# A tuned matmul-scale-add kernel: one 8-tile store split by partitions into 112, 8 and 8

## The chip, the cores and the metric

One core of a Trainium2 chip. The metric is the device time of one execution in microseconds; the kernel is launched once. Executions of the kernel before agree within about 0.4% in one set of rounds, so several timed rounds of both kernels on the same chip are compared.

## The reference

```python
batch, m, k, n = 16, 512, 1024, 768          # all float32
def reference(x, weight, scale, add_value):  # scale = 0.1
    return (scale * np.matmul(x, weight) + add_value).astype(np.float32)
```

The 8192 rows of `x` are 64 tiles of 128 rows. Read: 32 MiB of `x`, 24 MiB of `add_value`, 3 MiB of weights; written: 24 MiB.

## The kernel before

Everything comes and goes through DMAs between HBM (the main memory) and SBUF (the core's own memory, 128 partitions), which SyncE issues in the order of a list: loads of `x` ("x"), of the weights ("w"), of `add_value` ("a"), and stores of results ("o", then "l" and "r" for the two parts of the last tile). A result overwrites its `add_value` in the buffer `ao` and is stored from there. A partition holds eight consecutive rows of the output for a group of eight tiles, so an 8-tile store writes one run of 24,576 bytes from each of the 128 partitions. From here on such a run, one partition's part of an 8-tile store, is called a row.

```python
STREAM = [
    # ... (cut)
    ("o", 16, 8), ("o", 24, 8), ("a", 48, 8), ("x", 56, 8), ("a", 56, 8), ("o", 32, 8),
    ("o", 40, 8), ("o", 48, 8), ("o", 56, 4), ("o", 60, 1), ("o", 61, 1), ("o", 62, 1),
    ("l", 63, 1), ("r", 63, 1),
]
    # ... (cut)
    out_v = out_f.rearrange("(g p t) n -> p g t n", p=P, t=G)     # P = 128, G = 8
    # ... (cut)
        else:
            while done["step"] <= last:
                step()                       # compute up to this tile
            k = s % A_SLOTS
            n0, n1 = {"o": (0, N), "l": (0, CUT), "r": (CUT, N)}[op]
            nc.sync.dma_start(rows(out_v, s, n)[:, :, n0:n1], ao[:, k:k + n, n0:n1])
```

## Time and profile before

| | before |
|---|---|
| time, median of the first 3 runs | 210.86 us (210.78 to 211.06) |
| span of the profiled run | 209.2 us |
| last compute instruction ends | 204.03 us |
| TensorE busy | 196.4 us (94%) |
| bytes moved | 87.21 MB, 417 GB/s over the span |

Two resources are full nearly to the end, TensorE and the 16 DMA engines, and the last 5 us belong to the DMA engines alone. The prediction shows the lines for that. Here is what it doesn't show: the last 20 us of the kernel before in stretches of 4 us. The columns are named by the header; the last two are the share of time in which the 16 engines had a packet, and what they moved.

```profile
core 0: us, PE busy (x) PEld busy (x) DVE busy (x) ACT busy (x) POOL busy (x), PEclk, DMA share, GB/s
188.00:192.00 4.00, 4.00 (x28) 2.40 (x26) 1.19 (x2) 1.48 (x2) 0.00 (x0) 1.00 0.98 416
192.00:196.00 4.00, 4.00 (x28) 2.47 (x27) 1.68 (x2) 1.01 (x1) 0.00 (x0) 1.00 1.00 430
196.00:200.00 4.00, 4.00 (x29) 2.61 (x28) 0.96 (x1) 1.28 (x2) 0.00 (x0) 1.00 0.95 406
200.00:204.00 4.00, 3.57 (x22) 1.88 (x20) 2.04 (x3) 0.74 (x1) 0.00 (x0) 1.00 0.96 395
204.00:208.00 4.00, 0.00 (x0) 0.00 (x0) 0.04 (x1) 0.00 (x0) 0.00 (x0) 0.83 0.51 195
```

Read the last two columns as a pair. A share near 1 with 400 to 430 GB/s says that the engines are busy and go at full rate: in this trace a row mostly takes 912 ns, 26.9 GB/s, 431 for 16 engines. Both fall together after 204 us, as engines run out of work.

SyncE's own wait at the end of the program, for the stores to land (us in total, times, longest):

```profile
SPq L293 <- DMA out_dram<-ao: 3.7, 3, 2.8
```

### The profile page before, as it was taken

The page shows a single profiled execution, that of the slowest core. Times are in us where ns is not written, and L with a number is a line of the kernel's source. Part 1 is how long each engine was busy: PE and PEld are TensorE (multiplying, and loading weights), DVE is VectorE, ACT ScalarE, POOL GpSimd, SP SyncE. Part 2 cuts the span into 40 slices and gives each one's busy share as a digit, 9 for nine tenths or more (in the row PEclk, how much of TensorE's full clock was granted, in tenths as well). Part 3 has the DMA queues.
Part 4 walks back from the last instruction along what each step waited for, and adds up shares of the span by engine and source line. Part 5 has one row for each costly group of instructions (what it writes and reads, how often), then busy time and mean ns, then how long its engine had stood idle before and what let it go on. Part 6 is the DMA issues. An engine that isn't in the chain of part 4 may idle for free.

```text
span 209.2 us, 2988 instructions
## 1 busy us (share of the span) xinstructions
PE 196.4 (94%) x1218; PEld 119.5 (57%) x1218; DVE 131.1 (63%) x223; ACT 49.3 (24%) x52; POOL 63.2 (30%) x69
## 2 busy tenths in 40 slices
PE   7599499999999999999999999999999999999990
PEld 2355256656665666566665666565666656666550
DVE  0545413309969969898697886949994994223340
ACT  2513113233103112113032031121130230332310
POOL 1310536420292090503903606303503039100000
PEclk9889979999999999999999999999999999999997
DMA  6999999999999999999999999999999999999993
GB/s 233 418 431 447 423 408 441 451 445 407 404 481 410 418 432 418 432 451 415 437 417 436 436 421 425 442 434 423 423 432 445 445 409 418 432 447 426 409 402 152
DMA packets 5485, 87.21 MB, mean 417 GB/s; under 512 B 608, under 2 KB 736, under 8 KB 2016
## 3 DMA queue, kind: packets, MB, share of 16 engines
q1 hardware_dynamic: 5472, 87.03, 97.7%
q8 instruction: 9, 0.15, 0.3%
q14 instruction: 4, 0.03, 0.0%
HBM read 61.87 MB, written 25.17 MB: 416 GB/s over the span
## 4 chain that ended last, share of the span: by engine, by line
PE 90%; DMA 3%; DVE 2%; ACT 1%; POOL 0%; issue 0%; ACTq 0%; POOLq 0%
PE mm L168 80%; PE tp L146 10%; DMA xs<-in_x_dram 3%; DVE ao L235 1%; ACT xt L152 1%; DVE ao L204 1%; POOL xb L136 0%; DVE xb L132 0%; DVE ao L176 0%; ACTq L152 0%; POOLq L136 0%
## 5 line engine op out<-in xcount | busy, mean ns | idle before, releaser
L168 PE MATMUL mm<-w_bf,xt 128*128 128x512 bf16 (+1 forms) x736 | 130.8, 331 | 0.6 <-DVE ao L204 0.4
L168 PEld LDWEIGHTS <-xt 128*128 128x128 bf16 x736 | 69.6, 99 | 50.8 <-ACT xt L152 11.4
L176 DVE SCALAR_TENSOR_TENSOR ao<-mm,ao 128x768 f32<-128x768 f32 (+2 forms) x62 | 58.3, 944 | 54.1 <-PE mm L168 35.3
L152 ACT COPY xt<-tp 128x1024 bf16<-128x1024 bf16 (+1 forms) x49 | 46.6, 961 | 146.0 <-PE tp L146 146.0
L120 DVE STREAM_TRANSPOSE vt<-vx 32x256 f32<-32x256 f32 x144 | 62.7, 435 | 6.2 <-POOL vx L109 4.0
L136 POOL CAST xb<-xs 128x1024 bf16<-128x1024 f32 x43 | 43.2, 1040 | 56.2 <-DMA xs<-in_x_dram 46.5
L168 PE MATMUL mm<-w_bf,vt 128*128 128x512 bf16 (+1 forms) x288 | 49.7, 326 | 0.0
L168 PEld LDWEIGHTS <-vt 128*128 128x128 bf16 x288 | 28.2, 98 | 17.5
L109 POOL CAST vx<-xs 128x1024 bf16<-128x1024 f32 x18 | 18.3, 1040 | 53.8 <-DVE vt L120 44.7
L146 PE MATMUL tp<-identity,xb 128*128 128x128 f32 x184 | 28.3, 277 | 5.4 <-POOL xb L136 3.0
L146 PEld LDWEIGHTS tp<-identity,xb 128*128 128x128 f32 x184 | 21.7, 143 | 12.1 <-POOL xb L136 3.4
L104 DVE CAST w_bf<-ao 128x768 bf16<-128x768 f32 x8 | 4.1, 557 | 3.8 <-DMA ao<-in_weight_dram 3.8
L132 DVE CAST xb<-xs 128x512 bf16<-128x512 f32 x3 | 1.9, 696 | 5.6 <-DMA xs<-in_x_dram 5.6
L94 PE MATMUL warm<-zeros 128*128 128x512 bf16 x10 | 4.3, 617 | 1.2 <-DVE zeros L82 1.2
L134 POOL CAST xb<-xs 128x512 bf16<-128x512 f32 x2 | 1.6, 834 | 5.5 <-DMA xs<-in_x_dram 5.5
L94 PEld LDWEIGHTS <-zeros 128*128 128x128 bf16 x10 | 1.3, 140 | 3.4 <-issue 2.2
L204 DVE TENSOR_SCALAR ao<-mm 128x768 f32<-128x768 f32 x2 | 1.8, 952 | 2.3 <-PE mm L168 2.3
L235 DVE TENSOR_TENSOR ao<-ao 128x768 f32<-128x768 f32 x3 | 2.7, 950 | 0.0
L134 ACT CAST xb<-xs 128x512 bf16<-128x512 f32 x1 | 0.6, 618 | 4.8 <-DMA xs<-in_x_dram 4.8
L134 ACT ACT_TABLE_LOAD x1 | 1.3, 1283 | 0.7 <-PEq L279 0.7
L201 ACT ACTIVATE ao<-mm 128x768 f32<-128x768 f32 x1 | 0.8, 817 | 0.0
L82 DVE MEMSET zeros<- 128x256 uint32 x1 | 0.3, 272 | 0.9 <-PEq L279 0.9
(6 smaller groups left out, 0.9 us busy)
## 6 DMA issues: line engine op xcount, KB each, us to landing
xs<-in_x_dram SPq DMA_DIRECT2D x6, 4096.0 KB, 27.3
ao<-in_add_value_dram SPq DMA_DIRECT2D x7, 3072.0 KB, 24.3
out_dram<-ao SPq DMA_DIRECT2D x7, 3072.0 KB, 31.2
xs<-in_x_dram SPq DMA_DIRECT2D x3, 2048.0 KB, 22.0
ao<-in_weight_dram SPq DMA_DIRECT2D x4, 768.0 KB, 9.5
xs<-in_x_dram SPq DMA_DIRECT2D x1, 1536.0 KB, 6.0
ao<-in_add_value_dram SPq DMA_DIRECT2D x1, 1536.0 KB, 23.7
out_dram<-ao SPq DMA_DIRECT2D x1, 1536.0 KB, 11.7
```

The source lines that it names most:

```text
L94: nc.tensor.matmul(warm[:, 0:CUT], zeros[:, 0:P], zeros, start=True, stop=True)
L104: nc.vector.tensor_copy(w_bf[:, j + i, :], ao[:, s + i, :])
L109: nc.gpsimd.tensor_copy(vx[:, i, :], xs[:, (t0 + i) % X_SLOTS, :])
L120: nc.vector.transpose(vt[b:b + 32, :, 32 * a:32 * a + 32], pairs[32 * a:32 * a + 32, :, b:b + 32])
L134: other(xb[:, K // 2:K], src[:, K // 2:K])
L136: nc.gpsimd.tensor_copy(xb, src)
L146: nc.tensor.transpose(tp[:, c, :], pairs[:, c * P:(c + 1) * P], identity)
L152: nc.scalar.copy(dst[:, c:c + q, :, :], src[:, c:c + q, :, :])
L168: nc.tensor.matmul(mm_tiles[t, cols[0]][:, n0:n1], lhs(t, j), w_bf[:, j, n0:n1], start=(j == 0), stop=(j == KJ - 1))
L176: nc.vector.scalar_tensor_tensor(a, mm_tiles[t, part][:, n0:n1], float(scale), a, op0=mybir.AluOpType.mult, op1=mybir.AluOpType.add)
L204: nc.vector.tensor_scalar(ao[:, EARLY_AT + t, :], mm_tiles[t, BOTH[0]][:, 0:N], float(scale), None, op0=mybir.AluOpType.mult)
L235: nc.vector.tensor_add(ao[:, t, :], ao[:, EARLY_AT + t, :], ao[:, t, :])
```

## The change

The intent: at the end the 16 engines do not finish together. Engine completions for the three pieces: sixteen for the 112 rows, and eight for each 8-row piece. Shared out equally, that is nine rows of this store for eight engines and seven for the others, to let the others, taken to be late, catch up. The traces give no engine's number. The eight that complete the 8-row pieces are called the lower engines and the others the upper; these are names and say nothing more.

```diff
+SHARED = ("o", 40)
...
-            nc.sync.dma_start(rows(out_v, s, n)[:, :, n0:n1], ao[:, k:k + n, n0:n1])
+
+            cuts = [0, 112, 120, P] if (op, s) == SHARED else [0, P]
+            for p0, p1 in zip(cuts, cuts[1:]):
+                nc.sync.dma_start(
+                    rows(out_v, s, n)[p0:p1, :, n0:n1], ao[p0:p1, k:k + n, n0:n1])
```

## The prediction

> **What bounds the kernel now.** I read the page of the kernel before first: the slices of the span (second part), the DMA queues (third) and the chain that ended last (fourth). Then the waits of the DMA queue, the list of DMA issues with their time to landing, and last the end of the span cut into short stretches.
>
> The slices have all 16 DMA engines busy from the second to the last slice, at about 430 GB/s, and the DMA share of the stretches from 24 us to 180 us is 1.00 to 1.01. The page's queues add that besides the kernel's own transfers nine instruction fetches of 16 KB (q8)[...] ride on the same engines.
>
> ```profile
> DMA  6999999999999999999999999999999999999993
> GB/s 233 418 431 447 423 408 441 451 445 407 404 481 410 418 432 418 432 451 415 437 417 436 436 421 425 442 434 423 423 432 445 445 409 418 432 447 426 409 402 152
> q1 hardware_dynamic: 5472, 87.03, 97.7%
> q8 instruction: 9, 0.15, 0.3%
> q14 instruction: 4, 0.03, 0.0%
> ```
>
> TensorE is 94% busy as well, so two things end close together. Which of them ends last is read at the end of the chain (start, length, what), where the last work is a VectorE instruction:
>
> ```profile
> 199.64 3.95 PE mm L168 x24
> 203.59 0.02 issue
> 203.61 0.42 DVE ao L176
> ```
>
> The chain is over at 204.03 us; the span is 209.2 us. What follows is stores. The reader sees it in the stretches of the tail (length, busy time of PE, PEld, DVE, ACT, POOL, then clock, DMA share, GB/s):
>
> ```profile
> 204.00:205.00 1.00, 0.00 (x0) 0.00 (x0) 0.04 (x1) 0.00 (x0) 0.00 (x0) 1.00 0.94 373
> 205.00:206.00 1.00, 0.00 (x0) 0.00 (x0) 0.00 (x0) 0.00 (x0) 0.00 (x0) 1.00 0.78 293
> 206.00:207.00 1.00, 0.00 (x0) 0.00 (x0) 0.00 (x0) 0.00 (x0) 0.00 (x0) 0.83 0.26 94
> 207.00:208.20 1.20, 0.00 (x0) 0.00 (x0) 0.00 (x0) 0.00 (x0) 0.00 (x0) 0.50 0.05 17
> ```
>
> The share times 16 is the number of engines at work: 15, 12.5, 4, and then 0.8, that is one engine alone. The tail is not short of bandwidth, it waits for one late engine. The trace keeps the 16 completions of each DMA apart (without the engine's number). For the 8-tile store of tiles 48 to 55 they lie, before the last, at 3.45, 3.25, 3.13, 3.00, 2.80, 2.54, then 1.78, 1.77, 1.68, 1.66, 1.64, 1.57, 1.53, 1.29, 1.07 and 0 us. Up to 24.2 us the 16 are within 0.4 us of each other. At each of the nine q8 fetches one more engine falls back by about 1.5 us, and that at 189.9 us pushes one that was already among the last by another 1.3. So six engines lead by 2.5 us or more, and one is alone at the back.
>
> The list of issues says that the last store is not alone on its engines: 4.1 us to landing for one of 128 KB, of which those ahead of it in the queue are most (its first completion came 1.6 us after issue).
>
> ```profile
> out_dram<-ao SPq DMA_DIRECT2D x1, 256.0 KB, 4.4
> out_dram<-ao SPq DMA_DIRECT2D x1, 128.0 KB, 4.1
> ```
>
> [...]
>
> [...]
>
> [...]a row of 24,576 bytes took 912 ns in nearly every packet, 26.9 GB/s, whoever else was at work.[...]
>
> **The change, part by part.** No instruction of TensorE, VectorE, ScalarE or GpSimd changes in kind or order; only the line numbers move. SyncE gets two more issues.
>
> 1. Issue cost: two more at about 0.33 us (the stores' issues took 332 to 431 ns), at 157.8 us, where SyncE then waits until 180.5 for the next tiles. Nothing on the path: 0.
>
> 2. Semaphore slots: eight go round, and two more DMAs shift who shares. The two last stores (issued at 203.5 and 204.1) now come after the 112-row and the first 8-row piece in their slots. The store they replace landed at 193.6, 10 us earlier, so even a late landing by 8 us costs nothing.
>
> 3. Shares, as intended: [...]If the late engine is an upper one, it ends 0.91 us earlier. The next ones lead it by 1.07 to 1.78 us; an engine of the lower half among these, 0.91 later, ends up 0.2 to 0.9 us ahead of the old end. The gain is then 0.2 to 0.9 us, 210.0 to 210.7. If it is a lower one, the end moves out by 0.91 to 211.8.
>
> 4. [...]Together +4.6 to +7 us: 215.5 to 217.9.
>
> **The rivals.** (a) Balance works: item 3 with an upper late engine, about 210.2. For it: the late engines are few, the queue is backlogged up to the end, and whoever chose the lower engines for the extra share probably saw which are late; the ninth fetch fell on one that had been hit before[...]. Against it: item 4, and that the gain is capped by the next engines. (b) Balance the wrong way: 211.8. Nothing in the profile speaks for it in particular, but nothing excludes it, as the completions carry no engine number. (c) [...]215.5 to 217.9[...]. (d) The end hidden anyway: TensorE's chain ends at 204.03 and a store lands some 1.6 us after issue on a free engine, so no balance whatever brings the last landing under about 205.7, against 208.2 now; the most that could ever be won is 2.5 us, 1.2%. This rules out "faster by over 2%".
>
> **Range and chances.** I give [...]rival (a) 0.34, rival (b) 0.08. [...]That gives slower 0.55, same 0.43, faster 0.02. The figure is 216.0 us[...]; the range 209.8 to 221 takes in the balance that works[...], and nothing between is likely.
>
> **What would show it.** Step 3 would be right if packets of 24,576 bytes stay at 912 ns, the stretch from 207 us is gone and the last stores land within about 3.5 us of issue. Step 4 would be right if some 16 or more packets of that size take 3 to 4 us around 188 to 197 us, the GB/s of the last four or five slices fall well below 400, and the last small stores take 8 us or more to landing, with some engines then idle while eight are late. Steps 1 and 2 are wrong if TensorE's chain ends later than 204.1 us or SyncE waits for the store's pieces before the last two issues. The prediction is wrong as a whole if an 8-row piece runs at 27 GB/s for each of its eight engines[...].

Passages are cut from the prediction: the terms of step 4, the grounds of rival (c), and in step 3 how the rows were shared out (one row more for each lower engine, one less for each upper, 0.91 us each way by the trace's row). The sum came to 216.0 us. Step 4 was put at +4.6 to +7 us on top of the 210.9 before, 215.5 to 217.9, with a chance of 0.58; the figure stood in its lower part because rivals (a) and (b), 210.2 and 211.8, lie below it. What step 4 comes down to, and what the runs below test, is that the place of the small pieces costs time, because several engines read a few neighbouring partitions at once.

The fetches that it counts are these in the trace before: nine q8 packets of 16,384 bytes, each 1.0 to 1.1 us. After the first one engine's next completion came at 30.6 us, those of the other 15 by 29.1; after the ninth, at 189.9 us, one engine completed at 193.6 and the next at 192.3.

## The result, and the profile after

The changed kernel takes 219.88 us (median of 4, 218.25 to 220.14) against 210.82 for the kernel before in the same rounds: slower, by a ratio of 1.0417 (95% interval 1.0371 to 1.0463). Here and below a ratio is the mean time of one kernel's fast runs over that of the other's of the same rounds, so it is not quite the ratio of the medians.

The profiled run is the fastest of the changed kernel's, 218.25 us with a span of 216.5 us, so its trace shows some 7.3 us of the loss and not all 9. The slices of the changed kernel's page:

```profile
DMA  6999999999999999999999999999999999999952
GB/s 248 412 425 438 418 426 437 416 456 433 422 430 439 436 427 415 457 415 451 409 422 428 441 431 419 424 431 427 436 450 430 412 422 431 403 282 295 401 237 83
```

Up to the 35th slice the two kernels are alike; then two slices move 282 and 295 GB/s, although the row above still has nines. The same stretches of 4 us as before, for the changed kernel:

```profile
188.00:192.00 4.00, 4.00 (x28) 2.34 (x27) 1.46 (x2) 1.21 (x2) 0.00 (x0) 1.00 1.17 305
192.00:196.00 4.00, 4.00 (x29) 2.60 (x27) 1.42 (x2) 1.01 (x1) 0.00 (x0) 1.00 0.93 270
196.00:200.00 4.00, 4.00 (x28) 2.53 (x27) 0.96 (x1) 1.55 (x2) 0.00 (x0) 1.00 0.84 292
200.00:204.00 4.00, 3.30 (x21) 1.68 (x18) 2.07 (x3) 0.47 (x1) 0.00 (x0) 1.00 0.97 406
204.00:208.00 4.00, 0.00 (x0) 0.00 (x0) 0.00 (x0) 0.00 (x0) 0.00 (x0) 1.00 0.85 346
208.00:212.00 4.00, 0.00 (x0) 0.00 (x0) 0.00 (x0) 0.00 (x0) 0.00 (x0) 0.58 0.41 167
```

From 188 to 200 us the engines have packets (1.17, 0.93 and 0.84; over 1 because a packet counts where it starts) but move only 305, 270 and 292 GB/s. That is not idleness, it is slowness: each packet takes longer. The packet records of the trace show this (they, and the completions below, are read from the trace itself; no view prints them one by one). Before, nine rows in ten took 912 to 920 ns, and only 9 of 1,792 took over 1 us, the longest 1.57. In the changed kernel rows of 1.1 to 2 us begin at 184 us, with the 112-row piece, and twelve rows between 190 and 200 us took 2.7 to 5.3 us.

Twelve us at some 130 GB/s less than the kernel before (416, 430 and 406 against 305, 270 and 292) are 1.5 MB left over, 3.7 us of all 16 engines. But the loss is not shared by all 16. The trace has each engine's completion (without its number). For the store of tile 60 ten engines are done from 202.6 to 206.4 us, and six from 210.1 to 212.7. The two 8-row pieces show eight engine completions each, as was counted on; two engines are through the second piece by 194.3 us, and six only from 198.2 to 200.9. The six late completions of the store behind them (tiles 48 to 55) come 7.3 us after these, 205.5 to 208.2, which is eight rows of 912 ns: they are the same six. Six slow engines set the end, and the others run dry: after 208 us the share is 0.41, six or seven engines of 16.

The chain's last lines in the changed kernel (start, length, what):

```profile
199.37 3.95 PE mm L169 x24
203.34 0.42 DVE ao L177
```

Compute ends at 203.76 us, no later than before. All of the loss comes after it, and SyncE's wait for the stores at the end has grown accordingly:

```profile
SPq L298 <- DMA out_dram<-ao: 10.6, 5, 7.9
```

The times from issue to landing say the same of the small stores behind the split one. Before, then after (KB each, us):

```profile
out_dram<-ao SPq DMA_DIRECT2D x3, 384.0 KB, 7.4
```

```profile
out_dram<-ao SPq DMA_DIRECT2D x3, 384.0 KB, 15.0
out_dram<-ao SPq DMA_DIRECT2D x2, 192.0 KB
out_dram<-ao SPq DMA_DIRECT2D x1, 256.0 KB, 12.1
```

The 192 KB line is the two 8-row pieces; this view gives them no time.

### The profile page after: what moved, and what is told of

Same layout as the page of the kernel before. It is cut to its first block, busy times and chain, and to the rows that moved or that the text cites. A ratio compares the mean times of both kernels' runs of the same rounds, so it can differ in the third digit from the quotient of the medians.

```text
span 216.5 us, 2992 instructions
## 1 busy us (share of the span) xinstructions
PE 195.7 (90%) x1218; PEld 119.3 (55%) x1218; DVE 131.9 (61%) x223; ACT 49.3 (23%) x52; POOL 64.1 (30%) x69
## 4 chain that ended last, share of the span: by engine, by line
PE 67%; DMA 20%; DVE 5%; SPq 1%; issue 1%; ACT 0%; DVEq 0%; ACTq 0%
PE mm L169 60%; DMA ao<-in_add_value_dram 15%; PE tp L147 6%; DMA xs<-in_x_dram 5%; DVE vt L121 3%; DVE ao L177 2%; SPq L103 1%; ACT xt L153 0%; SPq L249 0%; DVEq L177 0%; ACTq L153 0%
## 5 line engine op out<-in xcount | busy, mean ns | idle before, releaser
L137 POOL CAST xb<-xs 128x1024 bf16<-128x1024 f32 x43 | 44.1, 1061 | 55.4 <-DMA xs<-in_x_dram 54.8
L147 PE MATMUL tp<-identity,xb 128*128 128x128 f32 x184 | 28.9, 283 | 5.0 <-DVE xb L133 2.6
L147 PEld LDWEIGHTS tp<-identity,xb 128*128 128x128 f32 x184 | 22.3, 146 | 11.2 <-issue 3.1
L95 PE MATMUL warm<-zeros 128*128 128x512 bf16 x10 | 3.6, 538 | 1.2 <-DVE zeros L83 1.2
L236 DVE TENSOR_TENSOR ao<-ao 128x768 f32<-128x768 f32 x3 | 3.5, 1231 | 0.0
```

The lines of the kernel that those rows point to most:

```text
L95: nc.tensor.matmul(warm[:, 0:CUT], zeros[:, 0:P], zeros, start=True, stop=True)
L137: nc.gpsimd.tensor_copy(xb, src)
L147: nc.tensor.transpose(tp[:, c, :], pairs[:, c * P:(c + 1) * P], identity)
L236: nc.vector.tensor_add(ao[:, t, :], ao[:, EARLY_AT + t, :], ao[:, t, :])
```

## The experiments

The theory ("neighbours"): several engines that read a few neighbouring partitions at the same time slow each other, so the place of the small pieces is the cost. Rivals: the engines' shares themselves are the cost (the lower eight carry too much); or the number of DMAs, their issues and their semaphore slots (in the trace before eight semaphores, used in turn, tell of the landings).

In the expectations the terms for this theory are cut; the figure behind a cut is what it came to. Cut as well are its opposites: extra_spread as slow as the packed run, extra_spread_up as fast as the spread run; of that for extra_four_ports the figure is left, 211.8.

All twelve kernels are the kernel before with an edit at the store of tiles 40 to 47.

| run | the store of tiles 40 to 47 | median us | before us | ratio (95% interval) |
|---|---|---|---|---|
| the change | 112 + 8 + 8 rows | 219.88 | 210.82 | 1.0417 (1.0371 to 1.0463) |
| tiles_4_2_2 | 4 + 2 + 2 tiles, 128 rows each | 211.00 | 211.21 | 0.9995 (0.9982 to 1.0008) |
| rows_112_16 | 112 + 16 rows | 214.36 | 211.21 | 1.0138 (1.0113 to 1.0163) |
| rows_64_64 | 64 + 64 rows | 216.33 | 211.21 | 1.0243 (1.0227 to 1.0259) |
| rows_8_8_112 | 8 + 8 + 112 rows | 215.94 | 211.03 | 1.0240 (1.0221 to 1.0258) |
| rows_112_only | 112 rows, the rest left out | 212.47 | 211.01 | 1.0074 (1.0061 to 1.0087) |
| shares_only | shares 9 and 7, 8-row pieces from every fourth partition | 210.95 | 211.01 | 0.9998 (0.9986 to 1.0010) |
| extra_spread | whole, and 2 x 8 rows, every fourth of partitions 0 to 29 | 211.73 | 211.03 | 1.0046 (1.0034 to 1.0059) |
| extra_spread_up | the same, every fourth of partitions 64 to 93 | 212.11 | 211.03 | 1.0063 (1.0045 to 1.0081) |
| extra_four_ports | the same, every second of partitions 0 to 15 | 213.57 | 211.01 | 1.0123 (1.0108 to 1.0138) |
| extra_low | the same, 8 neighbours each, partitions 0 to 15 | 213.43 | 211.01 | 1.0121 (1.0107 to 1.0135) |
| extra_packed | the same, 8 neighbours each, partitions 112 to 127 | 218.61 | 211.03 | 1.0359 (1.0346 to 1.0372) |
| extra_mid | the same, 8 neighbours each, partitions 64 to 79 | 219.24 | 210.93 | 1.0394 (1.0380 to 1.0408) |

What a run reads stands in the second column. A difference in us below is the ratio less 1, times the time before.

### Is it the number of DMAs? (tiles_4_2_2)

```diff
-            nc.sync.dma_start(rows(out_v, s, n)[:, :, n0:n1], ao[:, k:k + n, n0:n1])
+            cuts = [0, 4, 6, 8] if (op, s) == ("o", 40) else [0, n]
+            for t0, t1 in zip(cuts, cuts[1:]):
+                nc.sync.dma_start(
+                    rows(out_v, s + t0, t1 - t0)[:, :, n0:n1], ao[:, k + t0:k + t1, n0:n1])
```

> The same store cut into three DMAs as well, but by tiles (4, 2 and 2), each over all 128 partitions: the same number of issues and the same semaphore slots as in the change[...]. [...]within 0.5 us of before (210.3 to 211.3). Theory that the number of DMAs, the issues or the slots cost the 9 us: about 219. Shares theory (lower engines overloaded): 210.8, so this run parts only the count from the rest.

Measured: 0.9995, no difference, and no row of an 8-tile store over 1 us near the end. Three DMAs in the place of one, with the same shift of semaphore slots, cost nothing. That rival is out.

### Equal shares, fewer partitions (rows_112_16, rows_64_64)

```diff
+            cuts = [0, 112, 128] if (op, s) == ("o", 40) else [0, P]     # rows_112_16
+            cuts = [0, 64, 128] if (op, s) == ("o", 40) else [0, P]      # rows_64_64
```

> The store cut by partitions into 112 and 16[...], so no engine carries more than before. Shares theory: 210.8, as before. [...]+4.2 to +9 us, 215 to 220.

> The store cut by partitions into two halves of 64[...]. Shares theory: 210.8. [...]+4.8 to +7.3, 215.6 to 218.1, and the packets of 24,576 bytes take twice 912 ns, about 1.82 us.

Measured: +2.9 and +5.1 us. Both were meant to give every engine eight rows, as before, so the shares theory gave 0 for each. That the shares came out equal was not read from the traces. The theory had +4.8 to +7.3 for the halves, which holds; for 112 and 16 it had at least +4.2, which was too much: beside the 112-row piece alone (+1.6, below) the 16 rows cost some 1.3 us, 0.9 of it the row itself. In the trace of the halves 40 rows took 1.9 to 2.2 us, some twice the 912 ns, as expected. Three stretches of it (DMA share and GB/s at the end):

```profile
184.00:188.00 4.00, 3.95 (x28) 2.59 (x28) 0.96 (x1) 1.31 (x2) 0.00 (x0) 1.00 1.13 338
188.00:192.00 4.00, 4.00 (x27) 2.41 (x26) 0.96 (x1) 1.72 (x2) 0.00 (x0) 1.00 0.97 270
192.00:196.00 4.00, 3.95 (x26) 2.51 (x26) 1.87 (x2) 1.01 (x1) 0.00 (x0) 1.00 0.98 238
```

The engines are busy nearly throughout (share 1.13, 0.97 and 0.98) and move 282 GB/s on average, some two thirds of the 430 that full rate gives.

### Same bytes, same engines, other partitions (extra_packed, extra_spread, extra_spread_up)

Here the store stays whole and two stores of 8 rows to a spare tensor in HBM follow it. Between the three runs only the SBUF partitions differ; the targets, the sizes and the number of DMAs are the same, and the results are right.

```diff
+    spare = nc.dram_tensor("spare", (2, 8, G, N), fp32, kind="Internal").ap()
...
             nc.sync.dma_start(rows(out_v, s, n)[:, :, n0:n1], ao[:, k:k + n, n0:n1])
+            if (op, s) == ("o", 40):
+                for i, p in enumerate([slice(112, 120), slice(120, 128)]):      # extra_packed
+                # [slice(0, 32, 4), slice(1, 32, 4)]                            # extra_spread
+                # [slice(64, 96, 4), slice(65, 96, 4)]                          # extra_spread_up
+                    nc.sync.dma_start(spare[i], ao[p, k:k + n, :])
```

> The kernel before with its store whole, and behind it two more stores of 8 rows of 24,576 bytes into a spare tensor (the result stays right), partitions 112 to 119 and 120 to 127[...]. [...]+5 to +7.3, 215.8 to 218.1. Theory that only the added bytes count: 2 x 0.91 us on the lower engines, +0 to +1.8.

> The same two extra stores, same bytes, same engines, but from partitions 0, 4, ... 28 and 1, 5, ... 29[...]. [...]+0 to +0.2 us if the engine that ends last is an upper one, and +1.8 us if it is one of the lower eight. [...]So this run also tells which half the late engine is in.

> The same two extra stores from partitions 64, 68, ... 92 and 65, 69, ... 93[...]. [...]+1.8 us if the late engine is an upper one, up to +3.7 if a lower one.[...]

Measured: packed +7.6 us (just above its +5 to +7.3), spread +0.97, spread over partitions 64 to 93 +1.3. The first two are the cleanest pair. Packed, then spread:

```profile
188.00:192.00 4.00, 4.00 (x28) 2.37 (x26) 1.16 (x2) 1.50 (x2) 0.00 (x0) 1.00 1.30 373
192.00:196.00 4.00, 4.00 (x29) 2.47 (x27) 1.71 (x2) 1.01 (x1) 0.00 (x0) 1.00 0.92 246
196.00:200.00 4.00, 4.00 (x29) 2.64 (x28) 0.96 (x1) 1.25 (x2) 0.00 (x0) 1.00 0.78 283
```

```profile
188.00:192.00 4.00, 4.00 (x28) 2.37 (x26) 0.96 (x1) 1.83 (x2) 0.00 (x0) 1.00 0.97 410
192.00:196.00 4.00, 4.00 (x27) 2.47 (x27) 1.76 (x2) 1.01 (x1) 0.00 (x0) 1.00 1.00 430
196.00:200.00 4.00, 4.00 (x29) 2.65 (x27) 1.11 (x2) 1.01 (x1) 0.00 (x0) 1.00 0.97 415
```

The packed run shows the changed kernel's picture, the spread run that of the kernel before: nearly all its rows took 912 ns. Which partitions are read makes the difference between 1 and 7.6 us.

The spread run also tells where the late engine is. The eight engines of its first extra store complete it from 191.0 to 193.0 us; one row earlier, from 190.1 to 192.1, they had completed the whole store, whose last engine completed at 193.5. So the last engine is not among the eight. But four of the eight had completed only from 191.6 to 192.1, a lead of 1.5 to 1.9 us. Neither expectation for the spread run (0 to 0.2, or 1.8) had that mixture: two more rows, 1.82 us, on an engine that leads by 1.5 put it 0.3 to 0.4 us behind the former last; the run measured 0.7 to 1.2.

The third run missed its expectation of at least 1.8 us. Some rows took 1.0 to 1.6 us, but most stayed at 912 ns. So rows took twice as long in the halves and were hardly lengthened here; why, these runs do not tell.

### How close, and where (extra_four_ports, extra_low, extra_mid)

```diff
-                for i, p in enumerate([slice(112, 120), slice(120, 128)]):
+                for i, p in enumerate([slice(0, 16, 2), slice(1, 16, 2)]):      # extra_four_ports
+                # [slice(0, 8), slice(8, 16)]                                   # extra_low
+                # [slice(64, 72), slice(72, 80)]                                # extra_mid
```

> The two extra stores of 8 rows again, now from partitions 0, 2, ... 14 and 1, 3, ... 15[...]. Between the spread run ([...]+0.97) and the packed run ([...]+7.6). [...]+2 to +3.7 us, 212.8 to 214.7. [...]as the spread run, 211.8.

> The two extra packed stores from the low end, partitions 0 to 7 and 8 to 15[...]. [...]+5.8, 216 to 217.5. If the place does not matter: +7.6, 218.6.

> The two extra packed stores a last time, from partitions 64 to 71 and 72 to 79:[...] not the last 16 partitions. [...]near +7, 217 to 219. If the last 16 partitions are special: near the low run, 213 to 214. Either way above the spread run (+0.97).

Measured: +2.6, +2.55 and +8.3 us. Every second partition came out as expected. Neighbours at the low end cost no more than that, far under the +5.8 that I had expected, and neighbours in the middle somewhat more than at the high end (219.2 us, a little above the 217 to 219 expected). One stretch of the low and of the middle run:

```profile
192.00:196.00 4.00, 4.00 (x28) 2.48 (x26) 1.74 (x2) 1.01 (x1) 0.00 (x0) 1.00 0.97 369
```

```profile
192.00:196.00 4.00, 4.00 (x27) 2.48 (x26) 1.84 (x2) 1.01 (x1) 0.00 (x0) 1.00 1.08 264
```

So the last 16 partitions are nothing special. The two dear places, 64 to 79 (+8.3) and 112 to 127 (+7.6), lie in the upper half of the partitions, the cheap one, 0 to 15 (+2.55), in the lower. The upper half alone is not dear: the same bytes from every fourth partition of 64 to 93 cost +1.3. So it is closeness and place together. Why the place counts was not shown.

The low run also shows how little a packed store can suffer. The first engine completed the store before at 190.3 us, and the first extra store of 8 rows, 196,608 bytes, had landed on all eight engines at 193.1. By an estimate from these two times that is some 70 GB/s from eight neighbouring partitions, if no engine reads a row before it has finished the one before. The spread run completed the same store hardly earlier, at 193.0; only the second extra store lagged, 196.0 us against 193.9. In the packed run the same store landed from 192.6 to 196.4 us.

### The change taken apart (rows_112_only, shares_only, rows_8_8_112)

The first two give a wrong result: rows or a tile are not stored.

```diff
+            p1 = 112 if (op, s) == ("o", 40) else P                             # rows_112_only
+            nc.sync.dma_start(rows(out_v, s, n)[:p1, :, n0:n1], ao[:p1, k:k + n, n0:n1])
...
+            m = n - 1 if (op, s) == ("o", 40) else n                            # shares_only
+            nc.sync.dma_start(rows(out_v, s, m)[:, :, n0:n1], ao[:, k:k + m, n0:n1])
+            if (op, s) == ("o", 40):
+                for i, p in enumerate([slice(0, 32, 4), slice(1, 32, 4)]):
+                    nc.sync.dma_start(spare[i], ao[p, k:k + n, :])
...
+            cuts = [0, 8, 16, 128] if (op, s) == ("o", 40) else [0, P]          # rows_8_8_112
```

> The 112-row piece alone, the other 16 rows of this store left out (wrong result on purpose). Each engine has one row less: -0.91 us if seven rows to an engine run at full rate, 209.9. [...]+0.5 to +4 us, 211.3 to 214.8, with packets of 1.3 to 2 us at the time of this store.

> The intended shares[...] (wrong result on purpose: one tile is not stored, its bytes go elsewhere): the store covers seven of the eight tiles on all 128 partitions, and two stores of 8 rows of 24,576 bytes from partitions 0, 4, ... 28 and 1, 5, ... 29 go to a spare tensor. [...]If the intent was right[...]: -0.2 to -0.9 us, 210.0 to 210.6. If a lower engine ends last: +0.9. [...]nowhere near the 219.9 of the change.

> The change mirrored: pieces of 8, 8 and 112 rows from the low end, so the 8-row pieces come first[...]. Same shares as the change, same count. Shares theory (as intended): the same as the change's own intent, 210 to 211.8. [...]+5 to +13 us, 216 to 224.

Measured: +1.6 us, 0.0 us (neither of the two cases expected, -0.2 to -0.9 or +0.9) and +5.1 us.

The 112-row piece alone is 1.6 us slower than the whole store although, shared out equally over the sixteen completions that such a piece shows in the changed kernel's trace, each engine carries one row less (0.91 us). Seven rows to an engine thus lose 2.5 us against rows at full rate. Its stretch from 188 us (share, GB/s), with many rows of 1.1 to 2 us and two longer ones in the trace:

```profile
188.00:192.00 4.00, 4.00 (x28) 2.36 (x26) 1.05 (x2) 1.61 (x2) 0.00 (x0) 1.00 1.01 330
```

The two parts of the change add up: +1.6 for the 112-row piece and +7.6 for two packed 8-row pieces behind a store (extra_packed) make 9.1 us; the change itself measured 8.8 by its ratio (interval 7.8 to 9.8). Within that interval nothing else is needed to explain it. The mirrored split is the cheaper, in keeping with extra_low: 1.6 + 2.55 = 4.1 against 5.1 measured. It also puts its 8-row pieces first, so that it differs from the change in the order as well as in the place, and 1 us of it stays unexplained.

And the intent, without crowded partitions, is worth nothing: 0.9998, -0.3 to +0.2 us. The tail of shares_only:

```profile
206.00:207.00 1.00, 0.00 (x0) 0.00 (x0) 0.00 (x0) 0.00 (x0) 0.00 (x0) 1.00 0.33 125
207.00:208.20 1.20, 0.00 (x0) 0.00 (x0) 0.00 (x0) 0.00 (x0) 0.00 (x0) 0.74 0.08 29
```

There is still one straggler after 207 us. The eight lower engines had completed seven-eighths of the split store in two groups, the later one from 190.9 to 191.4, and complete their second extra row at up to 193.2, where the late upper engine had completed its share at 192.7. The last engine has changed sides.

No version that beats the kernel before came out of this. One would have to give the lower eight a little more without slowing the rows. shares_only does that (430, 449, 412 and 421 GB/s in the stretches of 4 us from 184 to 200, at shares of 1.00, 1.06, 0.96 and 0.98), at the price of a wrong result, and wins nothing with this half and half.

## Why the prediction was right or wrong

The direction and the class were right, and for the reason that had the greatest chance, the partitions of the small pieces (rival c). The figure of 216.0 was short by 3.9 us, and 219.9 lies above the 215.5 to 217.9 that step 4 was given.

- What bounds the end: right. Compute ends at 203.8 us, before it was 204.0, and all of the loss is in the stores that follow.
- Steps 1 and 2, issues and slots at no cost: right. tiles_4_2_2 has both and measured 0.9995; SyncE issued its last two stores at 203.2 and 203.8 us, before those of the kernel before.
- Step 3, the balance as intended, a gain of 0.2 to 0.9 us: its first case held, the last engine is an upper one (the spread run's completions), and so did its warning that some lower engines may stand among the next ones: four do. The gain is 0.0, at the low end less a little. Rival (a) falls with it, with crowded partitions or without; rival (b) too.
- Step 4, the place of the small pieces: right in kind, too small in size, +4.6 to +7 us against 8.8 measured (7.8 to 9.8). The 112 rows alone lost 2.5 us against full rate (rows_112_only, with the saved row added back), 1.6 in all, and two packed 8-row pieces cost 7.6 (extra_packed). The same theory gave +5.8 for extra_low, which measured +2.55, and at least +4.2 for rows_112_16, which measured +2.9. So it does not hold as a size, and that the figure came as near as it did owes something to luck.
- What would show it: the rows of 3 to 4 us came, fewer and longer than told (twelve of 2.7 to 5.3, from 190 to 200 us); the slices fell to 282 and 295 GB/s; the small stores took 12 to 15 us to landing; six engines were late where I had eight. The sign of being wrong as a whole, 27 GB/s for each of the eight engines of an 8-row piece, did not come: twelve rows took 2.7 us and more. The first piece of extra_low came nearest to it: the rows over 1 us that began from 189.8 to 192.1 us took 1.1 to 1.5 us, but for one of 2.4.

What stays open: why rows take twice as long in the halves and hardly longer in extra_spread_up, and why the low end is the cheaper place. That the choice of partitions sets the cost, with the same bytes, targets and number of DMAs, is shown (+0.97 against +7.6); what the engines share there is not.

## What to carry to other kernels

The store cut by tiles cost nothing here. Cut by partitions it cost 2.9 to 8.8 us, and two extra stores of eight neighbouring partitions each, 393 KB in all, cost 2.55 to 8.3. A high busy share of the DMA engines with a lower GB/s was the mark of it here (1.17 with 305): look at the two columns together. Before shifting work to "the early half", find out with a small extra transfer which engines are in it; here both halves held late ones, and the balance was worth nothing even where it was free.
